# A hybrid trunk's norms: a mean square made by one product in the blocks, and six factor vectors sent to all partitions by DMA

## The chip, the cores and the metric

One core of a Trainium2 chip runs the whole kernel. The time is the device time of one execution in microseconds, as the median over runs. TensorE is PE in the profile, VectorE is DVE, ScalarE is ACT, GpSimd is POOL, and SyncE (SP) only issues DMAs.

## The reference, cut to what matters

One layer, S = 2048 tokens of D = 1024, float32. Four RMS or layer norms matter here: before the projection, in mixer B, before the MLP, and at the end.

```python
def _rmsnorm(x, g):
    y = x * rsqrt(mean(x * x, -1) + 1e-6)
    return y * g
...
h = _rmsnorm(x, g_attn)
p = h @ w_in                      # mixers A, B and C's q, k, v
y_a = a_b * causal_dwconv(a_c * a_h, w_conv_a)            # width 3
g = glu * sigmoid(gate)                                   # mixer B
g = causal_dwconv(g, w_conv_b) + b_conv_b                 # width 31, 256 channels
y_b = silu(layernorm(g, ln_b_g, ln_b_b))
y_c = stick_breaking_attention(q, k, v)                   # 8 heads of 64
x = x + concat(y_a, y_b, y_c) @ w_out
h2 = _rmsnorm(x, g_ffn)
x = x + square(relu(h2 @ w_ff1)) @ w_ff2                  # 1024 -> 4096 -> 1024
return _rmsnorm(x, g_final)
```

## The kernel before

Activations are held with channels on the partitions and tokens along the free axis: a tile of 128 channels by TB = 512 tokens. The 2048 tokens are four token blocks of 512. Every large product is split: each float32 operand becomes a high and a low part in the type fp32r, and `mm3` (L103, L105, L107) adds three products, high by high, low by high and high by low. Products that stay in plain float32 are the small ones of the norms.

*Projection stage.* `p_half(0)` and `p_half(1)` project 1024 tokens each, unit by unit: gates, mixer A, keys, queries, values. `weave` advances side programs beside it, by a cost that each `yield` states: `mixer_b` (two token blocks per half; 31 conv taps on VectorE at L458, the mean product at L467, squares, column sum, `rsqrt`, then the multiply at L484, a sigmoid at L486 and a product on POOL at L488), `x_norms` (the norm factors of token blocks 2 and 3; blocks 0 and 1 have `norm_x`), the attention of block 0 and a splitting of later weights. The numbers behind each side in the calls of `weave` are its total cost and the stretch of the main program over which it is spent.

*Block stage.* For each token block, `block(tb)` makes the output product, adds x and sums the squares into `ss`, and then runs the MLP: `ffn1(c)` makes 128 hidden channels (L103 to L107 into `ps_u`), `ffn2(g)` adds groups of them into `ps_y`, which VectorE adds into `acc` (L984). The norm before the MLP is not applied to its input: since squared ReLU is homogeneous of degree two, the residual is multiplied by the mean square instead (L1008), and the last norm takes out the common factor; its epsilon is carried along in `em`. `finish_` makes the last norm.

*Norm factors.* `colsum` (L127) adds over the partitions with four plain float32 products of 128 x 2, so that the sums lie with tokens on the partitions, 128 x 4. `rsqrt` makes a factor with one VectorE instruction (L115 or L117) and a power on POOL (L118). `spread` (L134) brings such a 128 x 4 vector to all partitions along the free axis, with four plain float32 products of 128 x 128, into a PSUM bank `ps_R`. In the block, `mt` (L999) and `em` (L1001) are made from `colsum` and `mt` is spread.

PSUM has eight banks, which tags share: `d` three (main products), `z` two in the projection and three in the blocks, `c`, `q` and `o` one each. Loads go out on SP's queue, `dma` (L79) in program order, and some on POOL's (L83) and ScalarE's. The order of the instructions comes from the order of the code, from the costs in `weave` and from a scheduler that gives some parts a higher priority (`high_priority`); each queue keeps its order once it is set.

Of the kernel before, what the change touches and what calls it, by code (L numbers as in the profile page):

```python
# [7 lines left out]
F32 = mybir.dt.float32  # L8
# [20 lines left out]
RMS_EPS = 1e-6  # L29
LN_EPS = 1e-5  # L30

UNITS = ["G0", "G1", "A0", "A1", "A2", "K0", "K1", "Q0", "Q1", "V0", "V1"]
# [36 lines left out]
class Trunk:  # L69
# [39 lines left out]
    def rsqrt(self, ss, scale, eps, cols=slice(0, 4)):  # L109

        nc, pool = self.nc, self.tiny
        y = pool.tile([P, 4], F32, name="rs_y", tag="rs_y", bufs=6)
        v = pool.tile([P, 4], F32, name="rs_v", tag="rs_v")[:, cols]
        if isinstance(eps, float):
            nc.vector.tensor_scalar(v, ss[:, cols], scale, eps, op0=ALU.mult, op1=ALU.add)  # L115
        else:
            nc.vector.scalar_tensor_tensor(v, ss[:, cols], scale, eps[:, cols], op0=ALU.mult, op1=ALU.add)  # L117
        nc.gpsimd.tensor_tensor(y[:, cols], v, self.mhalf[:, cols], op=ALU.pow)  # L118
        return y
# [23 lines left out]

    def small(self, name, bufs=2):
        return self.tiny.tile([P, 4], F32, name=name, tag=name, bufs=bufs)


    def consts(self, ctx):
# [95 lines left out]
    def x_norms(self):  # L244

        for g in (2, 3):
            ss = self.mx.tile([P, TB], F32, name="ss", tag="ss", bufs=2)
            for d in range(DC):
                t = self.rp.tile([P, TB], F32, name="xraw", tag=self.rt, bufs=self.rb)
                self.dma(t, self.a["xT"][d * P : (d + 1) * P, g * TB : (g + 1) * TB])  # L250
                self.x_square(ss, t, d, self.nc.gpsimd)
                yield 1
            self.ss[g] = ss
            self.norm_sum(g)
            for _ in range(3):
                yield 1
            self.norm_spread(g)
            yield 1

    def norm_x(self, g):  # L260
# [186 lines left out]
    def mixer_b(self, hf):  # L447
        nc = self.nc
        for tb in (2 * hf, 2 * hf + 1):
# [404 lines left out]
    def block(self, tb, before):  # L854
# [107 lines left out]
        def ffn2(g, cols=slice(0, TB), ahead=0, again=0):  # L962
# [13 lines left out]
            for d in range(DC):  # L976
# [19 lines left out]
        need2(1)  # L996

        mt = self.small("mt")
        nc.vector.tensor_scalar(mt, self.colsum([ss], "z"), 1.0 / D, RMS_EPS, op0=ALU.mult, op1=ALU.add)  # L999
        em = self.small("em")  # L1000
        nc.vector.scalar_tensor_tensor(em, mt, RMS_EPS, mt, op0=ALU.mult, op1=ALU.mult)  # L1001
        yield from ffn1(2)
        need2(2)
        ms = self.spread(mt, "z")
        for d in range(DC):
            if d == DC // 2:
                yield from ffn1(3)
            nc.vector.tensor_tensor(acc[d], acc[d], ms, op=ALU.mult)  # L1008
        ss2 = hp.tile([P, TB], F32, name="ss2", tag="ss", bufs=1)
        sq7 = []  # L1010
# [8 lines left out]
        if tb < 3:  # L1019
            self.attend(tb + 1)  # L1020
            self.y_load(tb + 1, self.y_order(tb + 1)[: self.xb])
            yield from ffn2(FC // G - 1, ahead=2)
            self.end = self.finish_(tb, acc, [ss2], em)
        else:

            left, right = slice(0, TB // 2), slice(TB // 2, TB)
            yield from ffn2(FC // G - 1, left)
            fin = self.finish_(tb, acc, [ss2], em, left)
# [4 lines left out]
            self.finish(tb, acc, [ss2] + sq7, em, right)  # L1033
            for _ in fin:
# [6 lines left out]

    def finish_(self, tb, acc, sums, em, cols=slice(0, TB)):
# [17 lines left out]
    def build(self):  # L1060
        tc = self.tc
        with ExitStack() as ctx:
# [6 lines left out]
            with ExitStack() as c1:  # L1069
# [12 lines left out]
                self.ab = dict(Kl=1, A0=6, om=2, Alo=2, Ahi=2, Vl=1, late=1, yc=2)  # L1082
                weave(self.p_half(0), [(Side(self.mixer_b(0)), 115, 20, 225, True), (Side(self.x_norms()), 24, 60, 180, True)])
                self.heads = {}
                a0 = Side(self.attention([(h, 0) for h in range(H)]))
                weave(self.p_half(1), [(Side(self.mixer_b(1)), 116, 0, 200, True), (a0, 28, 0, 210, True), (Side(self.pre_split(self.presplit[:24])), 24, 0, 200, True), (Side(self.pre_split(self.presplit[24:])), len(self.presplit) - 24, 190, 230, True)])
            with ExitStack() as c2:
# [67 lines left out]
```

## Time and profile before

| what | value |
|---|---|
| median of 3 runs | 2396.46 us (2393.45, 2396.46, 2396.71) |
| profiled execution, its own time | 2389.55 us |
| its span | 2387.8 us |
| mean granted TensorE clock | 0.998 |
| PE, DVE, ACT, POOL busy | 99%, 63%, 45%, 48% |
| instructions on PE, DVE, ACT, POOL | 11316, 2492, 2002, 1231 |
| projection stage | to about 560 us of the span |

The busy times come from one profiled execution. PE's starts and ends are modelled and its matmuls overlap, so prices of its instructions are read from start to start. A plain float32 matmul appears as two records. In lists of instructions the first number is the start in us, the second the duration; what ended an engine's idle time stands in brackets behind an instruction.

### The profile page before, as it was taken

To read this page: it belongs to the slowest core of one execution; us is meant where nothing else is said; L and a number is where in the kernel's file an instruction comes from. 1 tells how busy PE (TensorE), PEld (TensorE's weight loads), DVE (VectorE), ACT (ScalarE), POOL (GpSimd) and SP (SyncE) were. 2 spreads that over 40 slices of the span, in tenths; PEclk is the share of its full clock that TensorE was granted. 3 is DMA by queue.
4 is the path that set the end of the run, shared out by engine and by line. 5 is a ranking of instruction groups with operands and counts; after the bars stand their busy time and mean duration, and the time that the engine had idled before them with its cause. 6 is when DMAs were issued, how large, how long until landed. Compare 5 with 4: busy or idle time off the path is not lost.

```text
span 2387.8 us, 32873 instructions
## 1 busy us (share of the span) xinstructions
PE 2369.9 (99%) x11316; PEld 2004.1 (84%) x11316; DVE 1500.4 (63%) x2492; ACT 1066.7 (45%) x2002; POOL 1151.7 (48%) x1231
## 2 busy tenths in 40 slices
PE   8999999999999999999999999999999999999998
PEld 7888988898888888888888888888888888888887
DVE  7966698943878777678766668586666525321114
ACT  5232433333566666545555555366555522311221
POOL 1342388731667666427666765278788710000000
PEclk9999999999999999999999999999999999999999
DMA  7569999888778777696677776856676557555545
GB/s 259 205 227 348 294 323 298 285 273 275 191 216 239 204 223 208 210 293 169 210 218 242 232 240 208 277 159 186 192 205 198 168 175 235 175 172 194 198 167 194
DMA packets 238984, 536.49 MB, mean 225 GB/s; under 512 B 27105, under 2 KB 100833, under 8 KB 223457
## 3 DMA queue, kind: packets, MB, share of 16 engines
q1 hardware_dynamic: 180304, 462.01, 57.9%
q0 software_dynamic: 39424, 62.93, 12.0%
q10 hardware_dynamic: 19088, 9.44, 1.4%
q8 instruction: 89, 1.46, 0.2%
q14 instruction: 79, 0.64, 0.1%
HBM read 386.19 MB, written 139.72 MB: 220 GB/s over the span
## 4 chain that ended last, share of the span: by engine, by line
PE 91%; DMA 3%; POOL 2%; issue 2%; DVE 1%; ACT 0%; SPq 0%; POOLq 0%; DVEq 0%; ACTq 0%
PE ps_u L103 10%; PE ps_y L103 10%; PE ps_u L105 10%; PE ps_u L107 10%; PE ps_y L105 10%; PE ps_y L107 10%; PE ps_p L107 4%; PE ps_p L105 3%; PE ps_p L103 3%; PE ps_z L528 3%; PE ps_z L529 3%; PE ps_x L107 2%; PE ps_x L103 2%; PE ps_x L105 2%; PE ps_o L735 2%; PE ps_o L734 2%
## 5 line engine op out<-in xcount | busy, mean ns | idle before, releaser
L90 POOL TENSOR_TENSOR Alo<-A,Ahi 128x512 fp32r<-128x512 f32 x288 | 383.7, 1343 | 90.5 <-ACT Ahi L88 54.3
L984 DVE TENSOR_TENSOR acc<-acc,ps_y 128x512 f32<-128x512 f32 (+1 forms) x264 | 176.0, 668 | 192.6 <-PE ps_y L107 190.2
L103 PE MATMUL ps_y<-fh,w 128*128 128x512 f32 (+1 forms) x1056 | 281.9, 385 | 0.0
L105 PE MATMUL ps_y<-fh,w 128*128 128x512 f32 (+1 forms) x1056 | 280.2, 384 | 0.0
L103 PE MATMUL ps_u<-hh,w 128*128 128x512 f32 x1024 | 278.9, 392 | 1.1 <-ACT hh L903 1.1
L107 PE MATMUL ps_y<-fl,w 128*128 128x512 f32 (+1 forms) x1056 | 279.7, 384 | 0.0
L105 PE MATMUL ps_u<-hh,w 128*128 128x512 f32 x1024 | 277.5, 390 | 0.0
L107 PE MATMUL ps_u<-hl,w 128*128 128x512 f32 x1024 | 277.1, 390 | 0.0
L623 POOL TENSOR_TENSOR A<-A,R 128x512 f32<-128x512 f32 x168 | 223.2, 1331 | 108.1 <-ACT A L621 90.8
L118 POOL TENSOR_TENSOR rs_y<-rs_v,mhalf 128x4 f32<-128x4 f32 (+1 forms) x13 | 13.2, 1017 | 480.5 <-DVE rs_v L117 437.7
L948 ACT ACTIVATE ps_u<-ps_u 128x512 f32<-128x512 f32 x128 | 74.6, 582 | 369.0 <-PE ps_u L107 362.1
L105 PEld LDWEIGHTS ps_y<-fh,w 128*128 128x128 f32 x1056 | 195.1, 188 | 39.6 <-DMA w<-wraw 0.4
L107 PEld LDWEIGHTS ps_y<-fl,w 128*128 128x128 f32 x1056 | 195.1, 188 | 38.8
L105 PEld LDWEIGHTS ps_u<-hh,w 128*128 128x128 f32 x1024 | 192.4, 188 | 40.5
L107 PEld LDWEIGHTS ps_u<-hl,w 128*128 128x128 f32 x1024 | 192.2, 188 | 39.9
L103 PEld LDWEIGHTS ps_y<-fh,w 128*128 128x128 f32 x1056 | 193.2, 188 | 36.5 <-DVE acc L984 0.2
L958 DVE TENSOR_TENSOR fl<-ps_u,fh 128x512 fp32r<-128x512 f32 x128 | 87.8, 686 | 210.6 <-ACT fh L957 210.1
L88 ACT ACTIVATE Ahi<-A 128x512 fp32r<-128x512 f32 x288 | 176.3, 625 | 92.7 <-PE ps_o L734 44.2
L103 PEld LDWEIGHTS ps_u<-hh,w 128*128 128x128 f32 x1024 | 187.5, 188 | 35.9 <-ACT hh L903 1.5
L625 DVE TENSOR_TENSOR R<-ps_z,R 128x512 f32<-128x512 f32 x168 | 115.7, 689 | 134.3 <-ACT ps_z L622 112.5
L458 DVE SCALAR_TENSOR_TENSOR ps_c<-g,wb,ps_c 128x512 f32<-128x512 f32 x240 | 180.1, 750 | 4.9
L90 DVE TENSOR_TENSOR w<-wraw,w 128x512 fp32r<-128x512 f32 x176 | 170.5, 993 | 19.4 <-ACT w L88 17.9
(179 smaller groups left out, 4749.0 us busy)
## 6 DMA issues: line engine op xcount, KB each, us to landing
w<-s_w SPq DMA_DIRECT2D x208, 512.0 KB, 4.0
wraw<-in_w SPq DMA_DIRECT2D x224, 256.0 KB, 4.7
w<-s_w SPq DMA_DIRECT2D x52, 1024.0 KB, 4.8
w<-s_w_out SPq DMA_DIRECT2D x64, 512.0 KB, 4.8
s_w<-w SPq DMA_DIRECT2D x48, 512.0 KB, 5.2
s_w<-w SPq DMA_DIRECT2D x24, 1024.0 KB, 5.9
Qd<-KQ SPq DMA_DIRECT2D x64, 256.0 KB, 6.1
xraw<-in_xT SPq DMA_DIRECT2D x48, 256.0 KB, 4.6
```

The source lines that it names most:

```text
L88: nc.scalar.activation(hi, x, AF.Copy)
L90: e.tensor_tensor(lo, x, f(hi), op=ALU.subtract)
L103: self.nc.tensor.matmul(ps, wh, xh, start=start and k == 0, stop=False)
L105: self.nc.tensor.matmul(ps, wl, xh, start=False, stop=False)
L107: self.nc.tensor.matmul(ps, wh, xl, start=False, stop=stop and k == n - 1)
L458: nc.vector.scalar_tensor_tensor(t, g[:, k : k + TB], self.wb[:, c, k : k + 1], t, op0=ALU.mult, op1=ALU.add)
L528: nc.tensor.matmul(z[:, oc], keys, g["qh"][:, qc], start=k == 0, stop=False)
L623: nc.gpsimd.tensor_tensor(t, t, R, op=ALU.mult)
L625: nc.vector.tensor_tensor(Rn, z, R, op=ALU.mult)
L948: nc.scalar.activation(ps, ps, AF.Relu)
L958: nc.vector.tensor_tensor(lo, ps, f(hi), op=ALU.subtract)
L984: nc.vector.tensor_tensor(acc[d][:, cols], acc[d][:, cols], ps, op=ALU.add)
```

## The change

In the projection, six factor vectors (those of `x_norms` for two token blocks and of `mixer_b` for four) no longer go through `spread`. `put_factors` writes the 128 x 4 vector to a small DRAM tensor NF on POOL's queue, and `all_factors` reads it back to all 128 partitions, 256 KB, on SP's queue, into a tile `R` or `Rc`; Rc takes a buffer of tag `sq`. The multiply of mixer B (L498 in the new file) reads Rc from SBUF, where it read a PSUM bank. In `mixer_b` there are now five yields between factor and read and three between read and multiply, where four stood between factor and spread; the costs in `weave` go from 115 and 116 to 123 and 124, and one end from 200 to 204.

In the blocks, the column sum, the two tiny VectorE instructions and the spread become one plain float32 product of `ss` by a constant matrix of 1/D, whose result stands in every partition (`ps_ms`, L1015). The residual is updated by one `scalar_tensor_tensor`, (ms + eps) * acc (L1021). The term `em` becomes a start value of the second sum of squares, made by ScalarE as Square(EM * ms + EM * eps) (L1017), so `square_sum` always adds, and `rsqrt` takes a plain number.

```diff
+EM = (D * RMS_EPS / P) ** 0.5
...
     def rsqrt(self, ss, scale, eps, cols=slice(0, 4)):
...
-        if isinstance(eps, float):
-            nc.vector.tensor_scalar(v, ss[:, cols], scale, eps, op0=ALU.mult, op1=ALU.add)
-        else:
-            nc.vector.scalar_tensor_tensor(v, ss[:, cols], scale, eps[:, cols], op0=ALU.mult, op1=ALU.add)
+        nc.vector.tensor_scalar(v, ss[:, cols], scale, eps, op0=ALU.mult, op1=ALU.add)
...
+        self.mean_d = c.tile([P, P], F32, name="mean_d")
+        nc.vector.memset(self.mean_d, 1.0 / D)
+        self.em_eps = c.tile([P, 1], F32, name="em_eps")
+        nc.vector.memset(self.em_eps, EM * RMS_EPS)
...
+        self.NF = [self.dr.tile([4, P], F32, name=f"NF{k}") for k in range(6)]
...
             self.norm_sum(g)
+            self.put_factors(g + 2, self.rv[g])
             for _ in range(3):
                 yield 1
-            self.norm_spread(g)
+            self.R[g] = self.mx.tile([P, TB], F32, name="R", tag="Rs", bufs=4)
+            self.all_factors(self.R[g], g + 2)
             yield 1
+
+    def put_factors(self, k, y):
+        self.nc.gpsimd.dma_start(self.NF[k].rearrange("b p -> p b"), y)
+
+    def all_factors(self, t, k):
+        self.dma(t, self.NF[k].rearrange("b p -> (b p)").unsqueeze(0).to_broadcast([P, TB]))
...
-            yv = self.rsqrt(self.colsum(sqs[:1], "c"), 1.0 / 256.0, LN_EPS)
-            for _ in range(4):
+            self.put_factors(tb, self.rsqrt(self.colsum(sqs[:1], "c"), 1.0 / 256.0, LN_EPS))
+            for _ in range(5):
                 yield 1.8
-            R = self.spread(yv, "c")
+            R = self.mx.tile([P, TB], F32, name="Rc", tag="sq", bufs=2)
+            self.all_factors(R, tb)
+            for _ in range(3):
+                yield 1.8
...
-    def square_sum(self, ss, t, d):
+    def square_sum(self, ss, t, d, begun=False):
...
-        if d == 0:
+        if d == 0 and not begun:
...
-                    self.square_sum(ss2[:, cols], acc[d][:, cols], d)
+                    self.square_sum(ss2[:, cols], acc[d][:, cols], d, begun=True)
...
-        mt = self.small("mt")
-        nc.vector.tensor_scalar(mt, self.colsum([ss], "z"), 1.0 / D, RMS_EPS, op0=ALU.mult, op1=ALU.add)
-        em = self.small("em")
-        nc.vector.scalar_tensor_tensor(em, mt, RMS_EPS, mt, op0=ALU.mult, op1=ALU.mult)
         yield from ffn1(2)
         need2(2)
-        ms = self.spread(mt, "z")
+        ms = self.psum("ps_ms", "z")
+        nc.tensor.matmul(ms, self.mean_d, ss, start=True, stop=True)
+        ss2 = hp.tile([P, TB], F32, name="ss2", tag="ss", bufs=1)
+        nc.scalar.activation(ss2, ms, AF.Square, bias=self.em_eps, scale=EM)
         for d in range(DC):
...
-            nc.vector.tensor_tensor(acc[d], acc[d], ms, op=ALU.mult)
-        ss2 = hp.tile([P, TB], F32, name="ss2", tag="ss", bufs=1)
+            nc.vector.scalar_tensor_tensor(acc[d], ms, RMS_EPS, acc[d], op0=ALU.add, op1=ALU.mult)
...
-        y = self.rsqrt(self.colsum(sums, "z", bs), 1.0 / D, em, b)
+        y = self.rsqrt(self.colsum(sums, "z", bs), 1.0 / D, 0.0, b)
...
-                weave(self.p_half(0), [(Side(self.mixer_b(0)), 115, 20, 225, True), ...
+                weave(self.p_half(0), [(Side(self.mixer_b(0)), 123, 20, 225, True), ...
...
-                weave(self.p_half(1), [(Side(self.mixer_b(1)), 116, 0, 200, True), ...
+                weave(self.p_half(1), [(Side(self.mixer_b(1)), 124, 0, 204, True), ...
```

Where instructions stand now is shown at four places; a row is the line, the operation, out<-in and the shape, and xN a run of equal rows.

TensorE in the first block, before, around the column sum (`ps_ss`); `ps_u` are ffn1's products, `ps_z` an attention product of the next token block:

```order
L528 MATMUL ps_z<-Qd,Kl 128x512
L529 MATMUL ps_z<-Qd,Kl 128x512
L127 MATMUL ps_ss<-ones_70,ss 128x2 x4
L103 MATMUL ps_u<-hh,w_6161 128x512 x4
L105 MATMUL ps_u<-hh,w_6161 128x512 x4
L107 MATMUL ps_u<-hl,w_6161 128x512
```

and some ten products later around the spread (`ps_R`), up to ffn2's first product (`ps_y`):

```order
L528 MATMUL ps_z<-Qd,Kl 128x512
L529 MATMUL ps_z<-Qd,Kl 128x512
L105 MATMUL ps_u<-hh,w_6163 128x512
L107 MATMUL ps_u<-hl,w_6163 128x512 x2
L134 MATMUL ps_R<-ident,mt 128x128 x4
L107 MATMUL ps_u<-hl,w_6163 128x512 x2
L103 MATMUL ps_y<-fh,w_6060 128x512 x4
```

The same engine after, at the place of the spread:

```order
L543 MATMUL ps_z<-Qd,Kl 128x512
L106 MATMUL ps_u<-hh,w_6147 128x512
L108 MATMUL ps_u<-hh,w_6147 128x512 x4
L110 MATMUL ps_u<-hl,w_6147 128x512
L1015 MATMUL ps_ms<-ss,mean_d 128x512
L110 MATMUL ps_u<-hl,w_6147 128x512 x3
L106 MATMUL ps_y<-fh,w_6054 128x512 x3
```

The column sum is gone, and one product of 512 columns stands three products ahead of the first `ps_y`, where the spread stood two ahead of it.

VectorE at the second mixer, where the first half of the projection ends, before (`xl` are the low parts of the second half's input, `vt` the values, `cb` the mixer's two channel tiles):

```order
L230 SCALAR_TENSOR_TENSOR xl_0_2309<-xraw,g_attn,xh_0_2308 128x512
L230 SCALAR_TENSOR_TENSOR xl_1_2315<-xraw,g_attn,xh_1_2314 128x512
L230 SCALAR_TENSOR_TENSOR xl_2_2321<-xraw,g_attn,xh_2_2320 128x512
L230 SCALAR_TENSOR_TENSOR xl_3_2327<-xraw,g_attn,xh_3_2326 128x512
L484 TENSOR_TENSOR cb_1618<-cb_1618,ps_R 128x512
L484 TENSOR_TENSOR cb_1902<-cb_1902,ps_R 128x512
L230 SCALAR_TENSOR_TENSOR xl_4_2333<-xraw,g_attn,xh_4_2332 128x512
L411 SCALAR_TENSOR_TENSOR vt<-ps_v,rs_y,vt 128x4x64
```

and after:

```order
L422 SCALAR_TENSOR_TENSOR vt<-ps_v,rs_y,vt 128x4x64 x4
L233 SCALAR_TENSOR_TENSOR xl_0_2299<-xraw,g_attn,xh_0_2298 128x512
L498 TENSOR_TENSOR cb_1661<-cb_1661,Rc 128x512
L498 TENSOR_TENSOR cb_1951<-cb_1951,Rc 128x512
L233 SCALAR_TENSOR_TENSOR xl_1_2305<-xraw,g_attn,xh_1_2304 128x512
L233 SCALAR_TENSOR_TENSOR xl_2_2311<-xraw,g_attn,xh_2_2310 128x512
L233 SCALAR_TENSOR_TENSOR xl_3_2317<-xraw,g_attn,xh_3_2316 128x512
L233 SCALAR_TENSOR_TENSOR xl_4_2323<-xraw,g_attn,xh_4_2322 128x512
```

The two multiplies stood behind four xl tiles, and stand behind one.

SP's queue at the same place before; WS holds split weights in DRAM, `xraw` is the input of the second half:

```order
L79 DMA WS<-wl_1904 128x2048
L79 DMA KQ<-klo 128x2x256 x2
L79 DMA xraw<-in_xT 128x512 x2
L79 DMA wl_2175<-WS 128x2048
L79 DMA wh_2176<-WS 128x2048
L79 DMA xraw<-in_xT 128x512 x9
```

and after:

```order
L82 DMA xraw<-in_xT 128x512 x2
L82 DMA wl_2176<-WS 128x2048
L82 DMA wh_2177<-WS 128x2048
L82 DMA Rc<-NF_82 128x512
L82 DMA xraw<-in_xT 128x512 x9
```

The broadcast read stands behind the two weight loads and ahead of the input loads of the second half.

POOL at the third mixer, from `rs_y`, the factor, to its put:

```order
L118 TENSOR_TENSOR rs_y<-rs_v,mhalf 128x4
L93 TENSOR_TENSOR Alo<-A_3384,Ahi 128x512
L93 TENSOR_TENSOR wpl<-wraw,wph 128x512
L593 TENSOR_TENSOR A_3668<-A_3668,om 128x256
L555 AFFINE_SELECT R<-R 128x256
L93 TENSOR_TENSOR wpl<-wraw,wph 128x512
L555 AFFINE_SELECT om<-om 128x256
L555 AFFINE_SELECT A_3733<-A_3733 128x512
L266 DMA NF_83<-rs_y 128x4x1
```

Seven pieces of other work stand between the two; before, the factor went from POOL straight to TensorE.

More of the change, by code (lines that the diff above doesn't have):

```diff
@@ L142, in psum_pool @@
         self.ps = ctx.enter_context(self.tc.tile_pool(name="ps" + str(banks["z"]), bufs=1, space=PSUM, reuse_waits="tile"))
-    def small(self, name, bufs=2):
-        return self.tiny.tile([P, 4], F32, name=name, tag=name, bufs=bufs)
     def consts(self, ctx):
@@ L1022, in block @@
             yield from ffn2(FC // G - 1, ahead=2)
-            self.end = self.finish_(tb, acc, [ss2], em)
+            self.end = self.finish_(tb, acc, [ss2])
         else:
@@ L1027, in block @@
             yield from ffn2(FC // G - 1, left)
-            fin = self.finish_(tb, acc, [ss2], em, left)
+            fin = self.finish_(tb, acc, [ss2], left)
             with self.tc.high_priority(offset=HP):
@@ L1032, in block @@
                         next(fin, None)
-            self.finish(tb, acc, [ss2] + sq7, em, right)
+            self.finish(tb, acc, [ss2] + sq7, right)
             for _ in fin:
@@ L1040, in finish, with finish_ @@
                 pass
-    def finish_(self, tb, acc, sums, em, cols=slice(0, TB)):
+    def finish_(self, tb, acc, sums, cols=slice(0, TB)):
         nc, a, hp = self.nc, self.a, self.hp
@@ L1082, in build @@
                 self.ab = dict(Kl=1, A0=6, om=2, Alo=2, Ahi=2, Vl=1, late=1, yc=2)
-                weave(self.p_half(0), [(Side(self.mixer_b(0)), 115, 20, 225, True), (Side(self.x_norms()), 24, 60, 180, True)])
+                weave(self.p_half(0), [(Side(self.mixer_b(0)), 123, 20, 225, True), (Side(self.x_norms()), 24, 60, 180, True)])
                 self.heads = {}
                 a0 = Side(self.attention([(h, 0) for h in range(H)]))
-                weave(self.p_half(1), [(Side(self.mixer_b(1)), 116, 0, 200, True), (a0, 28, 0, 210, True), (Side(self.pre_split(self.presplit[:24])), 24, 0, 200, True), (Side(self.pre_split(self.presplit[24:])), len(self.presplit) - 24, 190, 230, True)])
+                weave(self.p_half(1), [(Side(self.mixer_b(1)), 124, 0, 204, True), (a0, 28, 0, 210, True), (Side(self.pre_split(self.presplit[:24])), 24, 0, 200, True), (Side(self.pre_split(self.presplit[24:])), len(self.presplit) - 24, 190, 230, True)])
             with ExitStack() as c2:
```

## The prediction

> **What bounds the kernel now.** I read the page's first, second and fourth parts first, then TensorE's table of waits, then TensorE's timeline around every instruction that the change touches, and last the queues around the second mixer.
>
> ```profile
> PE 2369.9 (99%) x11316; PEld 2004.1 (84%) x11316; DVE 1500.4 (63%) x2492; ACT 1066.7 (45%) x2002; POOL 1151.7 (48%) x1231
> PE   8999999999999999999999999999999999999998
> PEclk9999999999999999999999999999999999999999
> PE 91%; DMA 3%; POOL 2%; issue 2%; DVE 1%; ACT 0%; SPq 0%; POOLq 0%; DVEq 0%; ACTq 0%
> ```
>
> TensorE is busy 99% of the span, in every slice, at full clock, and it carries 91% of the chain that ended last. A busy share of 99% does not by itself say that removed products shorten the time, so the next view is what TensorE ever waits for:
>
> ```profile
> PE ps_p L317 <- ACT wh L88: 6.3, 1, 6.3
> PE ps_u L103 <- ACT hh L903: 1.1, 1, 1.1
> PE ps_R L134 <- POOL rs_y L118: 1.1, 1, 1.1
> PE ps_ss L127 <- DVE ss L840: 0.9, 1, 0.9
> PE ps_z L528 <- DVE T L656: 0.7, 1, 0.7
> ```
>
> The columns are total, times and longest, in us. That is the whole table: about 10 us in 2388, of which 6.3 is the start. So TensorE's own instruction stream sets the time from the first weights to the end, and what leaves that stream leaves the time, unless a new wait replaces it.
>
> **The blocks.** TensorE around block 0's norm (start, duration, instruction, records; a plain fp32 matmul makes two records):
>
> ```profile
> 606.80 0.95 PE L127 MATMUL ps_ss<-ones,ss 128*128 128x2 f32 x8
> 607.61 1.17 PE L103 MATMUL ps_u<-hh,w 128*128 128x512 f32 x4
> 608.62 1.09 PE L105 MATMUL ps_u<-hh,w 128*128 128x512 f32 x4
> 609.54 0.40 PE L107 MATMUL ps_u<-hl,w 128*128 128x512 f32 x1
> ...
> 613.70 1.05 PE L134 MATMUL ps_R<-ident,mt 128*128 128x128 f32 x8
> 614.51 0.70 PE L107 MATMUL ps_u<-hl,w 128*128 128x512 f32 x2
> 615.06 1.09 PE L103 MATMUL ps_y<-fh,w 128*128 128x512 f32 x4
> ```
>
> Durations overlap, so I take prices from starts. Four ordinary products take 609.54 - 608.62 = 0.92. The column sum with four behind it takes 608.62 - 606.80 = 1.82, so the column sum costs 0.90. The spread with two products behind it takes 615.06 - 613.70 = 1.36, less 0.46 for the two: 0.90 again. Both go. What comes is one plain fp32 product of 512 columns. Its kind is in the trace already, in the mixer's mean, two at a time:
>
> ```profile
> 226.50 1.88 PE L467 MATMUL ps_mean<-cb,avg 128*128 128x512 f32 x4
> 227.82 0.68 PE L403 MATMUL ps_v<-wh,xh 128*128 128x256 f32 x1
> 228.34 0.28 PE L404 MATMUL ps_v<-wl,xh 128*128 128x256 f32 x1
> ```
>
> From 226.50 to 228.34 is 1.84; the one L403 of 256 columns in between is half an ordinary product, 0.12; two products are 1.72, one is 0.86. The far ends for it are 0.23 (an ordinary product of 512 columns, 0.92 / 4) and 1.05 (the spread's whole duration); I take 0.86, since that row has the same type and shape. A block saves 0.90 + 0.90 - 0.86 = 0.94, and four blocks 3.8; by the far ends 3.0 to 6.3.
>
> The rest of the block's edit lies on VectorE and ScalarE:
>
> ```profile
> L1008 DVE TENSOR_TENSOR acc<-acc,ps_R 128x512 f32<-128x512 f32 x32 | 19.6, 681 | 7.0 <-PE ps_R L134 7.0
> L1054 DVE SCALAR_TENSOR_TENSOR ot<-acc,g_final,ps_R 128x512 f32<-128x512 f32 x24 | 17.7, 747 | 39.5 <-PE ps_R L134 19.7 <-DMA outT<-ot 19.4
> L840 DVE TENSOR_TENSOR ss<-ss,sq 128x512 f32<-128x512 f32 x49 | 36.7, 750 | 13.5 <-ACT sq L839 13.4
> ```
>
> The eight multiplies become scalar_tensor_tensor of a bank: 747 instead of 681 ns, 0.5 us a block; the sum of squares adds one 0.75 us L840; two tiny instructions go. VectorE is busy 63% and the three banks of tag d cover it: in block 0 the product lands at about 614.4, eight updates end near 620.4, and the first ffn2 result, stored 3 x 0.92 = 2.8 us after 615.1, needs its bank back only when a fourth d tile starts, near 623. So nothing, with 2 to 3 us of cover; if that went, at most that overrun per block. ScalarE's one new Square per block is read only by the sums at the block's end, so nothing waits for it here; ScalarE is busy 45%. The last block adds one more half-width add on VectorE, off the final chain, which waits for TensorE there.
>
> **The projection.** Six spreads go, all between 140 and 498 us, and each costs what block 0's did:
>
> ```profile
> L134 PE MATMUL ps_R<-ident,rs_y x48: 269/275/276, 140.6 to 497.2; 128*128 128x128 f32 x48
> 252.12 1.05 PE L134 MATMUL ps_R<-ident,rs_y 128*128 128x128 f32 x8
> 252.93 0.36 PE L403 MATMUL ps_v<-wh,xh 128*128 128x256 f32 x1
> 253.13 0.28 PE L404 MATMUL ps_v<-wl,xh 128*128 128x256 f32 x1
> ```
>
> 48 records are 24 products, six spreads. From 252.12 to 253.13, less one L403, is 0.89; I take 0.90, so 5.4 us. Two ScalarE copies go too, which nothing on the chain waits for.
>
> In their place six factor vectors go through DRAM: a put of 512 four-byte pieces from POOL's queue, and a broadcast read of 256 KB on SP's. TensorE issues none of it, so the price is only what gets late. Behind the put stands POOL's next work, for an issue of about 0.6 us; behind SP's read stands SP's queue, which is held until the put has landed; behind VectorE's multiply by Rc stands its own queue. The second mixer is the tightest, because TensorE turns to the second half right behind it:
>
> ```profile
> 241.07 1.04 POOL L118 TENSOR_TENSOR rs_y<-rs_v,mhalf 128x4 f32<-128x4 f32 x1 [5.46 <-DVE rs_v L115]
> 261.64 1.19 POOL L490 DMA_DIRECT2D Y<-sq  x2
> 240.23 0.38 SPq L79 DMA_DIRECT2D wh<-WS  x1
> 251.34 8.11 SPq L79 DMA_DIRECT2D xraw<-in_xT  x8
> 250.56 2.74 DVE L230 SCALAR_TENSOR_TENSOR xl<-xraw,g_attn,xh 128x512 fp32r<-128x512 f32 x4
> 258.34 0.75 DVE L230 SCALAR_TENSOR_TENSOR xl<-xraw,g_attn,xh 128x512 fp32r<-128x512 f32 x1 [1.27 <-ACT xh L229]
> 268.18 1.07 PE L107 MATMUL ps_p<-xl,wh 128*128 128x512 f32 x4
> ```
>
> and the transfers to hold against it (KB, us from issue to landing):
>
> ```profile
> g_ffn<-in_g_ffn SPq DMA_DIRECT2D x1, 4.0 KB, 5.0
> xt<-in_xT SPq DMA_DIRECT2D x32, 256.0 KB, 3.9
> wh<-WS SPq DMA_DIRECT2D x11, 1024.0 KB, 9.1
> ```
>
> The factor is ready at 242.1. The put needs 0.6 (half of L490's 1.19 for two) and lands by the row of another small transfer 5.0 later, near 247.7; the read takes 3.9 to 9.1, I take 4.6 (the 256 KB row and a bit): Rc at about 252.3, at worst 256.8. VectorE now has the multiply behind the first xl, near 250.56 + 2.74 / 4 = 251.2, so it waits 1 us, at worst 5.6. SP's wait costs nothing: between 240.6 and 251.34 it had nothing to issue. VectorE's next xl tiles shift by the wait; the last one of the first product, at 258.34 + 0.75 = 259.1, is read by TensorE from 268.18: 9 us of cover. (It waits for ScalarE's xh, and in ScalarE's queue the sigmoid of the delayed channel stands ahead of that xh; this eats a part of the cover, an unknown one.) So nothing here: TensorE stalls only if Rc comes after 251.2 + 9 = 260, that is 18 us behind the factor instead of 10. The x_norms' two vectors have three yields, some 15 us, between put and read.
>
> The Trainium skill, page "DMA: Bandwidth & Descriptors" (sections "Anatomy of one DMA" and "Bandwidth"), counts a fixed 2 us for each DMA and about 10.5 ns for each packet. By it, as an estimate, a put of 512 pieces would be near 2 + 5.4 = 7.4 us and every Rc 2.4 us later than by the row of 5.0. The sum would stay as it is here, and the first rival below would get a chance of about 0.2. No row here has a write of such pieces.
>
> **Sum.** 5.4 + 3.8 = 9.2 us off TensorE's stream, no new wait. The profiled execution took 2389.55 us (span 2387.8): it would be 2380.4. The median of the three runs is 2396.46, 6.9 above the profiled one; from it, 2387.3.
>
> **Rivals.**
>
> Factors late (stall of 3 to 6 us). The third and fourth mixers run while VectorE, POOL and the DMA engines are near full:
>
> ```profile
> 262.00:300.00 38.00, 38.00 (x189) 32.25 (x188) 28.63 (x50) 17.07 (x36) 20.97 (x27) 1.00 0.97 323
> 300.00:360.00 60.00, 60.00 (x285) 50.20 (x284) 56.05 (x92) 23.41 (x50) 54.00 (x58) 1.00 0.93 317
> 360.00:420.00 60.00, 59.11 (x285) 48.37 (x284) 51.37 (x81) 23.14 (x45) 51.77 (x58) 1.00 0.94 301
> ```
>
> and the group of POOL's longest work:
>
> ```profile
> L90 POOL TENSOR_TENSOR Alo<-A,Ahi 128x512 fp32r<-128x512 f32 x288 | 383.7, 1343 | 90.5 <-ACT Ahi L88 54.3
> ```
>
> Columns are the window, its length, busy time of PE, PEld, DVE, ACT and POOL, clock, DMA share, GB/s. The DMA engines are busy 0.93 to 0.97 in all three, and from 300 to 420 VectorE is busy 86 to 93%. In the new order of the third mixer seven pieces of POOL's work stand between its rs_y and the put (up to 1.34 us each by the last row, so some 8 us); SP stands at Rc until the put has landed, and the weights behind it on SP come late; the transfer row of 9.1 instead of 3.9 would make VectorE wait 5. Against it: TensorE still idles only 0.9 us from 360 to 420. If two mixers each lose 1.5 to 3 us: 2390.3 to 2393.3.
>
> More than the sum. The table of waits has, besides the start, four waits of 1.1, 1.1, 0.9 and 0.7 us. Two end at a spread or a column sum, and another order of the work can close each of them. Three of the four: 2.7 more, 2384.6. Nothing in the trace says that it would.
>
> Slower. SP's read of Rc is one instruction in SP's order, behind a put which POOL must first reach. If in the third mixer POOL (51.77 of 60 busy) reaches it late, SP sends no weights for that long, and TensorE's product stands still once its prefetched tile is used up. With the 9 us of cover of the second mixer, a chain of 10 us may grow to 19 at no cost, and it decides when the stall passes 9.2 + 4.8 = 14 us, a chain of 33; at 35 the time is 2387.3 + 16 = 2403. For it: POOL's queue is where the put can be held up longest. Against it: seven pieces at 1.34 us are 9 of the 23 us that this takes.
>
> **How the numbers follow.** As forecast: 0.69, and by the prices' far ends between 2384.8 (5.4 + 6.3 off) and 2388.1 (5.4 + 3.0 off). Factors late: 0.17. More than the sum: 0.07. Slower: 0.07. A change of 0.2% (4.8 us) is about what a measurement of this kernel can tell from none, so faster means below 2391.7. About half of the late case lies below that: faster 0.69 + 0.07 + 0.08 = 0.84, same 0.09, slower 0.07. The range reaches over the late case, to 2393.3, and below to 2382.5, which is the case of more than the sum less 2 us for the spread of 3 us between the runs shown.
>
> **What the profile after would show.** No spread left between 140 and 498 us; one L1015 product a block, 0.86 us from start to start; a busy time of PE about 9 us lower; its waits still about 10 us in all, none with Rc or xl behind it; and a wait of VectorE before each mixer's multiply, 1 to 6 us. I would be wrong if TensorE's table of waits gained more than 4 us between 140 and 520, if the one product cost 1.8 rather than 0.86, or if TensorE stood at the start of ffn2 because the longer updates hold its banks.

## The result and the profile after

The changed kernel takes 2427.69 us (median of 4, 2425.57 to 2431.02) against 2395.53 for the kernel before (4 runs): a ratio of 1.0144, interval 1.0131 to 1.0156 (the bare quotient of the two medians is 1.0134). It is slower by 32 us where 9 us of gain were forecast. Its profiled span is 2425.7 us, 37.9 above the one before; that is more than 32, because the profiled execution before, at 2389.55 us, lies 6 us below its kernel's median.

The page of the changed kernel, the lines that answer to the first fence of the prediction:

```profile
PE 2373.6 (98%) x11212; PEld 1998.6 (82%) x11212; DVE 1525.5 (63%) x2491; ACT 1066.2 (44%) x2004; POOL 1155.1 (48%) x1237
PE 32%; issue 2%; DVE 1%; DMA 1%; ACT 0%; POOL 0%; POOLq 0%; DVEq 0%; ACTq 0%
```

104 records of TensorE are gone (52 products), yet its busy time rose by 4 us; a part of it now runs at a lower clock (below). The chain's shares of 32% tell little: it could be followed back only through a part of the span. The table of TensorE's waits (total, times, longest, us) says more:

```profile
PE ps_v L414 <- DVE vt L422: 19.4, 3, 8.5
PE ps_p L328 <- ACT wh L91: 6.6, 1, 6.6
PE ps_z L542 <- DVE R L592: 4.7, 4, 1.5
PE ps_p L106 <- DVE kq L389: 3.0, 2, 1.6
PE ps_u L106 <- ACT hh L917: 2.6, 2, 2.4
PE ps_z L542 <- DVE T L670: 2.0, 2, 1.1
PE ps_o L740 <- DMA Vd<-VS: 1.7, 1, 1.7
```

The whole table adds up to 45 us, against 10 before. The largest, 19.4 in three pieces, is new: TensorE's value products wait for VectorE to clear their banks. The three stand at 232, 276 and 541 us, each behind a put of factors.

**What VectorE waits for.** The wait that ended on the broadcast vector, in VectorE's waits:

```profile
DVE cb L498 <- DMA Rc<-NF: 30.0, 3, 12.1
```

At the second mixer, VectorE's timeline (the bracket is the idle time before, and what ended it):

```profile
261.40 0.75 DVE L233 SCALAR_TENSOR_TENSOR xl<-xraw,g_attn,xh 128x512 fp32r<-128x512 f32 x1
271.89 1.29 DVE L498 TENSOR_TENSOR cb<-cb,Rc 128x512 f32<-128x512 f32 x2 [9.74 <-DMA Rc<-NF]
273.10 2.73 DVE L233 SCALAR_TENSOR_TENSOR xl<-xraw,g_attn,xh 128x512 fp32r<-128x512 f32 x4
275.75 0.48 DVE L422 SCALAR_TENSOR_TENSOR vt<-ps_v,rs_y,vt 128x256 fp32r<-128x256 f32 x1
```

and TensorE's answer:

```profile
276.29 0.58 PE L414 MATMUL ps_v<-wh,xh 128*128 128x256 f32 x1 [6.81 <-DVE vt L422]
```

The multiply stands at the head of VectorE's queue for 9.7 us. Behind it is not only the xl that the prediction looked at, but a vt that clears a value bank: TensorE ran dry 7 us into the wait. VectorE's wait alone doesn't do it: at the first mixer, at 151 us, it stood for 8.2 us at the same multiply, and TensorE's next stall, 13 us later, was 1.5.

The first of the three stalls has no Rc in it. ScalarE's and POOL's rows ahead of it show that the split of the keys waits for buffers that earlier writes of keys (KQ) hold:

```profile
225.01 0.63 ACT L91 ACTIVATE khi<-kq 128x512 fp32r<-128x512 f32 x1 [7.57 <-DMA KQ<-khi]
```

```profile
227.06 1.54 POOL L93 TENSOR_TENSOR klo<-kq,khi 128x512 fp32r<-128x512 f32 x1 [7.30 <-DMA KQ<-klo]
```

In the code the value tiles (vt) take buffers of the same two tags as khi and klo, `hi` and `lo`. So ScalarE's first two value tiles wait as well, at 231.13 us 2.12 us for klo and at 232.92 us 1.31 us for a write of klo, and VectorE and TensorE wait behind them.

**Why Rc is late, and what else is.** Transfers of the changed kernel (KB, us from issue to landing):

```profile
Rc<-NF SPq DMA_DIRECT2D x4, 256.0 KB, 4.6
...
NF<-rs_y POOLq DMA_DIRECT2D x6, 2.0 KB, 11.3
```

The read is as forecast, 4.6. The put of 2 KB takes 11.3, not 5.0. Meanwhile other transfers suffer. The two views below are of ScalarE's writes of the values (VS) from 244 to 262 us, around the put at 253, and of the SP queue's writes and loads of keys and queries (KQ) from 196 to 213 us, around the x_norms' put at 199:

```profile
DMA to landing us min/median/max: 2.5/3.7/15.1
DMA to landing us min/median/max: 3.8/10.7/12.1
```

Before, where the same work stood some 6 to 10 us earlier (VS from 234 to 252, KQ from 190 to 207), the views had:

```profile
DMA to landing us min/median/max: 2.3/3.9/8.0
DMA to landing us min/median/max: 3.7/5.0/6.4
```

So while a put is under way, the KQ transfers take twice as long, and the VS writes at worst 15.1 instead of 8.0. In windows around the put of 253.1 us (last columns: clock, DMA share, GB/s):

```profile
255.00:258.00 3.00, 3.00 (x27) 3.00 (x26) 0.57 (x2) 0.47 (x1) 0.00 (x0) 1.00 1.03 363
258.00:262.00 4.00, 4.00 (x35) 4.00 (x34) 1.48 (x3) 1.72 (x4) 0.00 (x0) 1.00 1.41 141
262.00:266.00 4.00, 4.00 (x36) 4.00 (x35) 0.15 (x1) 1.82 (x3) 0.00 (x0) 1.00 0.87 62
```

The DMA engines stay busy (the share is the time that packets took and can pass 1) and move 62 GB/s instead of 363: 2 KB hold them up for some 8 us. Around the put at 199 they move 40 GB/s from 203.3 to 209.8 us.

**What a stall costs on top.** The window of TensorE's own clock right behind the stalls that end at 232 and 276:

```profile
232.00:239.00 7.00, 6.82 (x31) 5.86 (x32) 0.61 (x2) 0.47 (x1) 0.00 (x0) 0.69 0.99 370
276.00:281.00 5.00, 4.71 (x23) 4.71 (x24) 4.54 (x6) 4.55 (x11) 4.99 (x7) 0.52 0.95 297
```

The granted clock is 0.69 and 0.52 there, 1.00 before. Over the span it is 0.993 instead of 0.998: of 2426 us that is 17 us of full clock missing, against 5. Of these 12 us more, some 5 fall inside the three stalls, where TensorE does nothing anyway (0.65 from 223.70 to 232.18 us, 0.83 from 269.48 to 276.29, 0.89 from 536.90 to 541.07); some 7 slow its work behind them (0.50 from 232.18 to 236.00, 0.67 from 276.29 to 283.00, 0.57 from 541.07 to 548.00). So the balance of the two spans is 35 us more of waits, 7 more of lost clock, less 9 for the products removed: 33 of the 37.9. The other 5 us are not accounted for. The Trainium skill, page "TensorE: Matmul & The Clock Gate" (section "What's actually happening"), has TensorE fall to half its clock after an idle window of about 3.4 us; the trace agrees for the three long stalls. Shorter ones can do it too: in e1, below, a stall of 2.4 us was followed by a clock of 0.55 from 1544.0 to 1547.5 us.

### The profile page after: what moved, and what is told of

It reads as the page before. It is cut to its first block, busy times and chain, and to the rows that moved or that the text cites. A ratio compares the mean times of both kernels' runs of the same rounds, so it can differ in the third digit from the quotient of the medians.

```text
span 2425.7 us, 32692 instructions
## 1 busy us (share of the span) xinstructions
PE 2373.6 (98%) x11212; PEld 1998.6 (82%) x11212; DVE 1525.5 (63%) x2491; ACT 1066.2 (44%) x2004; POOL 1155.1 (48%) x1237
## 5 line engine op out<-in xcount | busy, mean ns | idle before, releaser
L110 PE MATMUL ps_y<-fl,w 128*128 128x512 f32 (+1 forms) x1056 | 279.8, 384 | 0.6 <-DVE fl L972 0.6
L110 PE MATMUL ps_u<-hl,w 128*128 128x512 f32 x1024 | 277.9, 390 | 0.0
L110 PEld LDWEIGHTS ps_y<-fl,w 128*128 128x128 f32 x1056 | 195.0, 188 | 39.7 <-DVE fl L972 1.0
L110 PEld LDWEIGHTS ps_u<-hl,w 128*128 128x128 f32 x1024 | 192.2, 188 | 40.3 <-issue 0.5
L93 DVE TENSOR_TENSOR w<-wraw,w 128x512 fp32r<-128x512 f32 x176 | 182.9, 1063 | 25.9 <-ACT w L91 23.8
L91 ACT ACTIVATE w<-wraw 128x512 fp32r<-128x512 f32 x176 | 105.5, 627 | 179.7 <-PE ps_y L110 139.0
```

Source lines behind the costliest of these rows:

```text
L91: nc.scalar.activation(hi, x, AF.Copy)
L93: e.tensor_tensor(lo, x, f(hi), op=ALU.subtract)
L110: self.nc.tensor.matmul(ps, wh, xl, start=False, stop=stop and k == n - 1)
```

## The experiments

All ratios are against the kernel before, run on the same chip in the same session; the interval is 95%.

**Parts.** e1 is the blocks' part alone, e2 the projection's part alone.

```diff
-            self.put_factors(tb, self.rsqrt(self.colsum(sqs[:1], "c"), 1.0 / 256.0, LN_EPS))
-            for _ in range(5):
+            yv = self.rsqrt(self.colsum(sqs[:1], "c"), 1.0 / 256.0, LN_EPS)
+            for _ in range(4):
                 yield 1.8
-            R = self.mx.tile([P, TB], F32, name="Rc", tag="sq", bufs=2)
-            self.all_factors(R, tb)
-            for _ in range(3):
-                yield 1.8
+            R = self.spread(yv, "c")
```

This is e1's edit of the changed kernel in mixer_b; x_norms and the weave numbers go back in the same way. e2 is the kernel before with the same lines turned the other way.

> The blocks' part alone: the projection has its six spreads, its yields and its weave costs as before. By the prediction's term (0.94 us a block, PE only) 2395.5 - 3.8 = 2391.7, ratio 0.9984. Rival: the small new waits of TensorE seen behind 600 us in the changed kernel (about 6 us together) belong to the blocks' part and eat it: 2395 to 2398, ratio 1.000 to 1.001.

> The projection's part alone; the blocks have column sum and spread as before. If all of the loss sits in the projection and the blocks bring their 3.8: 2427.7 + 3.8 = 2431.5, ratio 1.015. If the blocks' part carries a third or more of the loss: 2417 or below, ratio under 1.009.

e1: 2391.81, ratio 0.9996 (0.9986 to 1.0005). e2: 2426.70, ratio 1.0148 (1.0135 to 1.0161). The whole loss is the projection's. The blocks bring 1 us, not 3.8: 0.9984 lies just outside the interval. Their price was right: in e1's timeline 1.55 us pass from 612.35 to 613.90, three products L110 take 0.69 of it, and the new one 0.86.

```profile
612.35 1.02 PE L1010 MATMUL ps_ms<-ss,mean_d 128*128 128x512 f32 x2
612.81 1.26 PE L110 MATMUL ps_u<-hl,w 128*128 128x512 f32 x3
613.90 0.85 PE L106 MATMUL ps_y<-fh,w 128*128 128x512 f32 x3
```

But small waits came in the blocks (e1's table of TensorE's waits, without the rows that stayed):

```profile
PE ps_u L106 <- ACT hh L912: 2.7, 2, 2.4
PE ps_z L537 <- DVE T L665: 2.2, 2, 1.3
...
PE ps_y L106 <- DVE acc L993: 0.9, 2, 0.4
...
PE ps_y L110 <- DVE fl L967: 0.6, 1, 0.6
```

Against 1.1 and 0.7 in the first two groups before, these are 4.6 us more. The 0.9 at ps_y looks like what the prediction named as a way to be wrong, that the longer updates hold the banks. It is not: the eight updates take 4.87 us, as the eight multiplies before did, and the first of the two waits comes 23 us after ffn2's first product, right behind a weight split that kept VectorE for 5.58 us:

```profile
614.13 4.87 DVE L1016 SCALAR_TENSOR_TENSOR acc<-ps_ms,acc 128x512 f32<-128x512 f32 x8 [0.89 <-ACT ss L1012]
630.85 5.58 DVE L93 TENSOR_TENSOR w<-wraw,w 128x512 fp32r<-128x512 f32 x1
637.08 1.20 PE L106 MATMUL ps_y<-fh,w 128*128 128x512 f32 x4 [0.41 <-DVE acc L993]
```

The same kind of split, by L90, stood there before and took 2.77 us; what stretched it is not known. The second wait, at 1638 us, comes behind twelve products of attention on VectorE (L697, 7.26 us), some 73 us after that block's updates. So no row ties these small waits, or the 2.8 us that the blocks fall short, to the change.

**The put alone.** e3 keeps the six spreads and still issues the six puts; nothing reads them.

```diff
 yv = self.rsqrt(self.colsum(sqs[:1], "c"), 1.0 / 256.0, LN_EPS)
+self.put_factors(tb, yv)
 ...
 R = self.spread(yv, "c")
```

> The blocks' part as changed; the projection multiplies by the six spreads as before, with the yields and weave costs of before, but the six puts of 512 four-byte pieces are still issued and nothing reads them. Theory A (the pieces hold up the DMA engines for all transfers, some 8 us each): waits of TensorE for evacuations remain, 6 to 20 us over the blocks' part alone, 2398 to 2412, and other transfers issued during a put land in 10 us instead of 5. Theory B (only VectorE's wait behind the late Rc costs): no wait, no loss: 2391.7, like the blocks' part alone.

2412.56, ratio 1.0083 (1.0070 to 1.0096): 0.87% or 21 us over e1, 3.5 a put, for 12 KB that nobody waits for. Theory B, that only VectorE's wait behind Rc costs, falls. The order of e3 differs from that of e1 in some places, which by itself can cost some 5 us (e13, below), not 21. The waits are the same kind as in the changed kernel:

```profile
PE ps_v L413 <- DVE vt L421: 8.6, 4, 3.6
```

**Number of pieces.** e4 turns the vector first, so that the put has 4 pieces of 512 bytes; e6 puts 128 pieces of 16 bytes. The instructions of e6 stand in the changed kernel's order on every engine and move the same bytes.

```diff
...
+ps = self.psum("ps_T", "c" if k < 4 else "o")
+self.nc.tensor.matmul(ps[:4, :P], y, self.ident, start=True, stop=True)
+self.nc.scalar.activation(t[:4, :P], ps[:4, :P], AF.Copy)
-self.nc.gpsimd.dma_start(self.NF[k].rearrange("b p -> p b"), y)
+self.nc.gpsimd.dma_start(self.NF[k], t[:4, :P])
```

and e6:

```diff
-self.nc.gpsimd.dma_start(self.NF[k].rearrange("b p -> p b"), y)
+self.nc.gpsimd.dma_start(self.NF[k].rearrange("b p -> (b p)").rearrange("(p b) -> p b", b=4), y)
```

> The changed kernel, but each factor vector is first turned by one plain fp32 product with the identity (128 x 4 to 4 x 128) and copied by ScalarE, so that the put is 4 pieces of 512 bytes instead of 512 of 4 bytes; queues, reads, yields and order numbers as changed. Theory A (the pieces): the put lands in about 4 to 5 us, Rc's waits shrink from 30 to under 6 us, and the time is 2395.5 - 9.2 + 6 x 0.22 = 2387.6, ratio 0.997. Theory C (the other order of the work, from the weave's numbers and the yields, makes the loss): it stays above 2410.

> The changed kernel with the put laid out as 128 pieces of 16 bytes instead of 512 of 4; the factors arrive in another order of tokens, so the output is not the reference's, all instructions and bytes are the same. Theory A (the number of pieces): the put lands after about 4.5 + (11.3 - 4.5) / 4 = 6.2 us, and the time falls most of the way to that of 4 pieces, 2400 to 2410. Rival (a put from the software queue is slow whatever its pieces): 11 us and 2427.

e4: 2399.44, ratio 1.0030 (1.0019 to 1.0041). e6: 2398.07, ratio 1.0021 (1.0010 to 1.0032). The transfers, first of e6, then of e4:

```profile
NF<-rs_y POOLq DMA_DIRECT2D x6, 2.0 KB, 6.0
```

```profile
NF<-sq POOLq DMA_DIRECT2D x4, 2.0 KB, 4.6
NF<-ss POOLq DMA_DIRECT2D x2, 2.0 KB, 4.4
```

The same 2 KB land in 11.3 us as 512 pieces, 6.0 as 128 and 4.5 as 4. (The number of pieces is read off the kernel. On POOL's queue the trace counts 32 packets for a put in all three; on ScalarE's, in e7 below, it counts 496 more for each, of under 512 bytes.) From the changed kernel to e6 only the size of the pieces differs, and 1.23% or some 29 us go. The waits for vt, 19.4 in the changed kernel, are in e6

```profile
PE ps_v L414 <- DVE vt L422: 2.0, 3, 0.9
```

and behind the second mixer's put the DMA engines move 304 and then 184 GB/s (247 to 251 and 251 to 255 us), where the changed kernel had 141 and 62. So the size of the pieces is the cause of nearly the whole loss. Short puts don't reach the forecast, though: 2387 was expected of e4, with under 6 us of waits for Rc, and VectorE still waits 10.1 there. What is left is taken up below. The Trainium skill, page "DMA: Bandwidth & Descriptors", bears on this in two places (section "Rules for kernel authors": a last dimension that isn't contiguous becomes one descriptor for each element; section "Specifications": below 512 bytes the engine reads, modifies and writes). The runs agree in that pieces set the time; that other transfers are held up by it is seen in the runs above alone, and no run shows whether reading and modifying is the reason.

**The queue.** e7 issues the changed kernel's put from ScalarE's queue.

```diff
-self.nc.gpsimd.dma_start(self.NF[k].rearrange("b p -> p b"), y)
+self.nc.scalar.dma_start(self.NF[k].rearrange("b p -> p b"), y)
```

> The changed kernel with the 512 pieces put on ScalarE's queue instead of POOL's. Theory A (the pieces hold up the DMA engines, whoever issues them): landing stays 9 us or more and the time 2420 to 2432. Rival (POOL's software queue is what is slow): the put lands in about 5 us and the time is 2400 to 2410.

2434.72, ratio 1.0170 (1.0156 to 1.0184), a little above the range given, and the put lands in

```profile
NF<-rs_y ACTq DMA_DIRECT2D x6, 2.0 KB, 9.8
```

So POOL's queue is not to blame for more than 1.5 us of the landing, and for none of the loss.

**Where the put costs.** e15 puts a constant four times; e16 puts 4 columns of each block's `ss`, so that the put can't leave its block. Nothing reads either; both have the blocks' part and six spreads.

```diff
+        self.put_factors(tb, self.mhalf)
         ms = self.psum("ps_ms", "z")
```

```diff
+        self.put_factors(tb, ss[:, 0:4])
         ms = self.psum("ps_ms", "z")
```

> The blocks' part, all six spreads kept; in each of the four blocks one put of 512 four-byte pieces (a constant, which nothing reads) on POOL's queue, ahead of the block's mean-square product. Theory A says the DMA engines are held there too, some 8 us a put; whether TensorE feels it depends on the weights loaded ahead (DMA share 0.6 to 0.77 there, against 0.93 in the projection). If loads ahead cover it: 2391 to 2393. If not: 3.5 us a put as in the projection, 2405.

> As the run before with puts in the blocks, but each put takes its 512 pieces from the block's own sums of squares, so that the scheduler can't move it to the program's start; nothing reads it. Theory A with cover (weights loaded ahead bridge the hold-up of some 8 us): 2391 to 2394, ratio 1.000. Without cover: about 3.5 us a put as in the projection, 2405.

e15: 2406.95, ratio 1.0062 (1.0050 to 1.0074). It can't answer the question: the scheduler issued all four puts within the first 5 us, where they landed in 18 us and TensorE's wait for its first weights grew from 6.3 in one piece to 14.7 in two. e16: 2414.56, ratio 1.0076 (1.0056 to 1.0095), 4.8 a put over e1. Its waits and the view of its puts:

```profile
PE ps_u L106 <- DMA w<-s_w: 14.3, 4, 4.8
```

```profile
L264 POOL DMA_DIRECT2D NF<-ss x4: 767/767/830, 592.5 to 2051.5; - x4
DMA to landing us min/median/max: 11.2/11.4/11.6
```

The weights loaded ahead don't bridge the hold-up: TensorE waits up to 4.8 us for a weight, and the clock falls, as in this window behind the stall that ends at 1564:

```profile
1564.00:1570.00 6.00, 6.00 (x15) 4.72 (x16) 0.00 (x0) 0.68 (x2) 0.00 (x0) 0.59 0.63 212
```

**What is left with short puts.** e8 has e4's put, but four yields in all and weave's numbers of before. e9 and e10 send only the norms' or only the mixers' vectors by e4's put. e11 sends only the norms' vectors, by the changed put.

The edit of e8; e9 to e11 put the other part back to spreads as in e1:

```diff
-            for _ in range(5):
+            for _ in range(1):
                 yield 1.8
             R = self.mx.tile([P, TB], F32, name="Rc", tag="sq", bufs=2)
```

> The put of 4 pieces of 512 bytes, but four yields in all between factor and multiply (one ahead of the read, three behind it) and the weave's numbers of the kernel before. If the order of the change costs: 2390 to 2396, lower than the 2399 of the run with 4 pieces. If the lateness of Rc costs: VectorE waits longer for Rc than the 10.1 us of that run, and the time is 2400 to 2410.

> The blocks' part; only the two x_norms vectors go through DRAM, as 4 pieces of 512 bytes; the mixers spread as before, with the yields and weave numbers of before. If what is left in the run with 4 pieces sits in the mixers (their reads on SP's queue and their order): 2391.8 - 2 x 0.68 = 2390.4, ratio 0.999. If it sits in the norms' part: 2396 or more.

> The blocks' part; only the mixers' four vectors go through DRAM, as 4 pieces of 512 bytes, with the yields and weave numbers of the change; the x_norms spread as before. If what is left sits in the mixers: 2397 to 2401, as with all six. If it sits in the norms' part: 2391.8 - 4 x 0.68 = 2389.

> The blocks' part; only the two x_norms vectors go through DRAM, with puts of 512 four-byte pieces as changed; the mixers spread as before. Theory A (each such put holds up the DMA engines): two puts at 20.8 / 6 = 3.5 us each by the run with puts alone, so 2391.8 + 7 = 2399 and no wait for R. Theory B (only a consumer that waits for the vector costs; R is not urgent): 2390.

e8: 2400.09, ratio 1.0031 (1.0019 to 1.0042). Neither of its cases came out: the time is that of a late Rc, but VectorE waits only 5.5 us for Rc, less than the 10.1 of e4. e9: 2405.86, 1.0059 (1.0046 to 1.0071). e10: 2402.63, 1.0045 (1.0033 to 1.0057). e11: 2412.11, 1.0085 (1.0072 to 1.0098). The split failed: each half alone with short puts is slower than both. From e9 to e11 the two puts go from 4 to 512 pieces, which costs 0.26%, 3 us a put (their orders differ too), and brings the wait for vt that the changed kernel has at 232:

```profile
PE ps_v L414 <- DVE vt L422: 4.7, 1, 4.7
```

In e9 the changed code ends at about 215 us and nothing waits for R; its stalls stand 120 us and more later, at work that no edit touched:

```profile
337.26 0.39 PE L740 MATMUL ps_o<-Ahi,Vd 128*128 128x256 f32 x1 [2.99 <-ACT Ahi L91]
366.11 0.58 PE L542 MATMUL ps_z<-Qd,Kd 128*128 128x256 f32 x1 [5.02 <-DVE R L592]
```

**Order alone.** e5 has all six spreads and no transfer of factors, but the change's yields and weave numbers. e13 and e14 have the blocks' part and all spreads, with weave's numbers at 118 and 119, or with two yields instead of three in x_norms.

The edits of e5 (against e1; weave's numbers are those of the change) and of e14:

```diff
             yv = self.rsqrt(self.colsum(sqs[:1], "c"), 1.0 / 256.0, LN_EPS)
-            for _ in range(4):
+            for _ in range(8):
                 yield 1.8
             R = self.spread(yv, "c")
```

```diff
-            for _ in range(3):
+            for _ in range(2):
                 yield 1
             self.norm_spread(g)
```

and of e13, in the calls of weave (shown for the first half):

```diff
-(Side(self.mixer_b(0)), 115, 20, 225, True)
+(Side(self.mixer_b(0)), 118, 20, 225, True)
```

> The blocks' part as changed, all six spreads kept on TensorE and no factor through DRAM, but the mixers with the eight yields between factor and multiply and the weave's numbers 123, 124 and 204 of the change. Theory A (put and read make the loss): like the blocks' part alone, 2391 to 2393 (ratio 1.000). Theory C (the later multiply and the other order cost by themselves): 2399 to 2407, a ratio of 1.003 or more, which would be what is left in the run with 4 pieces.

> The blocks' part, all six spreads kept, the same instructions; only the mixers' two cost numbers in weave are 118 and 119 instead of 115 and 116, which makes the scheduler put the work beside the projection in a slightly other order. Theory D (the order before is a tight one, and any other order of the third and fourth mixers' stage costs some us): 2396 to 2405, ratio 1.002 or more. Rival (orders are alike, and what is left in the runs with short puts is the price of the DMA route itself): 2390 to 2394, ratio 0.999 to 1.001.

> The blocks' part, all six spreads kept; only x_norms has two yields instead of three between factor and spread, so its two spreads stand a little earlier. Theory D: 2395 to 2404. Rival: 2390 to 2394.

e5: 2415.24, ratio 1.0093 (1.0079 to 1.0108). It is no clean test of order: the last mixer's spread came to the end of the stage, POOL's loads for the next stage stood behind its product, and TensorE waited for them:

```profile
PE ps_z L537 <- DMA Kd<-KQ: 13.3, 1, 13.3
PE ps_x L106 <- ACT y L91: 6.6, 1, 6.6
```

Neither wait is in the changed kernel. e13: 2397.06, ratio 1.0017 (1.0008 to 1.0026), 5 us over e1 with the same instructions; one stall of 3.0 us at 362, where e9 has its 5.0. e14: 2394.47, ratio 1.0006 (0.9998 to 1.0015), which can't be told from e1. So another order may cost some 5 us, and the stage from 330 to 430 us is where it shows. That may explain a part of the 11 us by which e6 lies above e1 less the spreads' 5.4; the rest, and e9's 15, are not settled: the reads, the 12.8 us for which VectorE still waits for Rc in e6, and an unlucky order could each be in it.

**A way without DMA.** e12 makes the mixers' factors in every partition by one product, as the blocks do, with POOL's power over 512 columns.

```diff
+var = self.psum("ps_var", "c")
+self.nc.tensor.matmul(var, self.avg, sqs[0], start=True, stop=True)
 R = self.mx.tile([P, TB], F32, name="Rc", tag="sq", bufs=2)
+nc.vector.tensor_scalar(R, var, 1.0, LN_EPS, op0=ALU.mult, op1=ALU.add)
+nc.gpsimd.tensor_tensor(R, R, self.mhalf[:, 0:1].to_broadcast([P, TB]), op=ALU.pow)
```

> The blocks' part; x_norms spread as before; each mixer makes its factor without column sum, spread or DMA: one plain fp32 product of the squares by the matrix of 1/256 (0.86 us) leaves the variance in every partition, VectorE adds the epsilon (0.7 us) and POOL takes the power over 128 x 512. TensorE saves 0.94 a mixer: if POOL's power of 512 columns takes about what its other work of that width takes (1.3 us), 2391.8 - 3.8 = 2388, ratio 0.998. If POOL's power is slow per element, POOL (86% busy there) and the multiply come late: 2400 or more.

2664.46, ratio 1.1145 (1.1129 to 1.1161). The power takes 82 us each:

```profile
L491 POOL TENSOR_TENSOR Rc<-Rc,mhalf 128x512 f32<-128x512 f32 x4 | 327.8, 81954 | 3.1 <-DVE Rc L490 3.1
```

No run is clearly faster than the kernel before; e1 equals it.

## Why the prediction was wrong, by its steps

- *The bound and the prices of the products* held: TensorE sets the time, one plain product costs 0.86 (e1), and the spreads are gone.
- *"TensorE issues none of it, so the price is only what gets late."* This step failed. The put was priced as its own delay. But a put holds up the other transfers: six puts that nobody reads cost 21 us (e3), four in the blocks 19 (e16), and 128 pieces instead of 512 take some 29 us out of the changed kernel (e6).
- *"The put needs 0.6 and lands by the row of another small transfer 5.0 later."* That term was mis-sized: 11.3 at the median. The row taken was a single load of 4 KB; nothing in the trace wrote 512 pieces. The sum by the page's figure gave 7.4, nearer and still short, and neither has the effect on others.
- *"9 us of cover" at the second mixer* was read along xl alone. The vt behind the same multiply clears TensorE's value bank and had 7 us. Rc came 19 us behind the factor (252.8 to 271.9), where the prediction allowed 18, and the stall was 6.8. And the x_norms' two vectors, thought covered by the 15 us between put and read, made the longest stall (8.5 us, at 232), by way of the keys' writes, which land in 10.7 instead of 5.0 us; e11, with these two puts alone, has a stall of 4.7 there, and e9, with short ones, none. The cover was for the reader of the vector, and the loss came to others.
- *The blocks' 3.8* came to 1 (e1; the interval reaches from a gain of 3.4 to a loss of 1.2). The longer updates were not the reason: priced at 747 ns each, they took 678 at the median, against 681 for the multiplies before. ScalarE's Square does hold something up: by the profile the updates wait for it (5.9 us in three waits), but they waited as much for the spread before (7.0 in two). The small waits of TensorE that came in the blocks are not tied to one row of the change, and why the gain fell short stays open.
- *Half clock behind a stall* was not in the sum at all: some 7 us of TensorE's work.
- *The rivals.* The slower one had the right sign and a chance of 0.07. It named SP's hold and weights that come late, at the third mixer and from a chain of 33 us on. The chain there was 24.5 (factor at 407.8, Rc landed at 432.3), and VectorE did not even wait for it; the three long stalls stand behind other puts. The rival of late factors saw VectorE's wait, at half of its size (5 us, against 9.7 and 12.1 at the second and fourth mixers). What the prediction called the sign of being wrong, more than 4 us of new waits between 140 and 520 us, is what came: 8.5 at 232 and 6.8 at 276.

## What to carry to other kernels

Count the pieces of a transfer, not its bytes: here a 2 KB write in 512 pieces held up the DMA engines for about 8 us, so its price is what the other transfers lose in that time, whether or not anyone waits for it. Turning the data first (e4) or writing runs of 16 bytes (e6) took most of that price away. Take the cover of a wait along every instruction behind it in the same queue, and the first consumer that runs dry sets it. In this kernel, at 99% of TensorE, each of the three long stalls cost 2 to 3 us again in clock, and a change of order alone cost 5 us (e13), half of what the edit was meant to bring.

## What the runs showed of the hardware that was not expected

- A put of 2 KB to DRAM landed in 11.3 us as 512 pieces of 4 bytes, 6.0 as 128 of 16 and 4.5 as 4 of 512; from ScalarE's queue 9.8 as 512. During the 512 pieces the DMA rate fell from 363 to 62 GB/s, and writes on other queues took up to 15.1 us.
- POOL's power took 1.0 us for 128 x 4 and 82 us for 128 x 512: about 0.16 us for each column.
- A stall of 4.4 us was followed by a granted clock of 0.59 over the next 6 us (e16), one of 2.4 us by 0.55 over 3.5 us (e1).
